# Order of the context stages and priority of the weight splits in a hybrid RWKV-7 and Conformer backbone

## The chip, the cores and the metric

The kernel runs on one core of one Trainium2 chip. The metric is the device time of one execution in microseconds (us). Three executions of the kernel before took 1431.3, 1439.53 and 1440.98 us; the median is 1439.53.

## The reference

The kernel computes two layers over 512 latent tokens of width 1024, with 256 context tokens as a prefix, all in float32. Layer 0 normalises both streams, projects them with one wide matrix, runs RWKV-7 time mixing in both directions beside a short gated convolution, and projects back. Layer 1 is a Conformer convolution module on the latent tokens. What matters here is the even layer, cut to its core:

```python
def even_mixer(h, hc, ...):
    rc, kc, vc, ... = split(hc @ w_in)              # context tokens: keys and values are used
    _, S_f, S_b = rwkv_seq(rwkv_prep(hc, rc, kc, vc), zero, zero, ctx_out=False)
    r, k, v, za, bg, cg, xb, zb = split(h @ w_in)   # latent tokens
    ya, _, _ = rwkv_seq(rwkv_prep(h, r, k, v), S_f, S_b, ...)
    yb = bg * dwconv(cg * xb, sc_w)
    return concat([ya * silu(za), yb * silu(zb)]) @ w_out

def wkv_scan(S, r, decay, k, v, kk, a):             # one step a token, 16 heads of 64
    S = S * w_t + (S @ -kk_t) (kk_t * a_t)^T + v_t k_t^T
    out_t = S r_t
```

The context's scans give only the states S_f and S_b with which the latent scans start. So for a context token only keys and values are projected (and the two low-rank decays), and no output is made.

## The kernel before

**Pairs and stages.** The 16 heads are eight pairs of two, since two heads of 64 fill 128 partitions. The recurrence is worked in chunks of 64 tokens. The context has four chunks, and two pairs of heads are done together as one context state, so there are four context states (0 to 3); the latent tokens have eight chunks and one state for each of eight pairs. These twelve states are the stages of one loop (`for s in range(12)`, the end of the list of calls): stages 0 to 3 run a context state's chain, 4 to 11 a latent one's. Names in the profile that end in c belong to context states, those that end in l to latent ones (AR becomes ARc and ARl).

**What one state needs,** in the order in which its data flow:
- `prep_ctx` (L397): projections of keys and values for two pairs. `project` (L376) loads a weight block of 1024 x 128, multiplies the context rows with it (24 matmuls of 256 columns, tile pck or pcv) and the latent rows (24 of 512, plk or plv), and mixes each token with its neighbours in `shifted` (L368: one ACT and two DVE instructions, L370, L371, L373). The latent result goes to HBM (psp) for later; `prep_lat` (L407) only reads it back.
- `light` (L431): normalised keys, decays and rates, on VectorE and ScalarE with a few matmuls (ssc, lwc, lac), twice over for the two directions. It ends in the tiles AR and BK.
- `heavy` (L589): V transposes and centres the values into UV (`pv`: pvc), B transposes BK (pbc to BKt), A makes the pair products of each chunk (pac or pal) and masks them on VectorE into E (L610), N copies blocks of E into Nt, O is for latent states alone.
- `solve` (L653): 31 double steps on VectorE alone (L667, L669), a triangular inverse of all chunks at once, after a transpose of Nt.
- `merge` (L672): two transposes on VectorE and two groups of 64 small matmuls (uh<-amc, uh<-kdmc) that complete the inverse in E. It takes buffers of light (tags kd, a, P, one buffer each).
- the chain: `chain_ctx` (L698) or `chain_lat` (L749), the sequential part, chunk after chunk. One step of the context's chain is two or three groups of 16 matmuls (zoc, zoc<-cx), copies on ScalarE, 16 matmuls into uh and four instructions on VectorE that give the next state H.

**Weights.** All projections are float32 by three passes: each weight half (128 x 512) is loaded by SyncE's queue into a raw buffer (L125), cast on ScalarE to a high half (L128), and the rest subtracted on VectorE into a low half (L129). `w_half` (L352) does this; there are two raw buffers, and three of each half. A projection's two psum banks are mm0 and mm1 in turn, one buffer each.

**Fills.** `fills(x)` (L908) are projections that no one needs soon: receptances `project(p, 0)` (plr) and gates `gate` (L797, pza), which go to HBM for the latent stages. FILL_R and FILL_Z say which belong to which x: fills(0) R0, R1, Z0; fills(1) Z1 to Z3; fills(2) R2; fills(3) R3, Z4 to Z7; fills(4) R4 to R7. `conv_branch(0)` with four projections follows the last context stage.

**What sets the order.** The program is scheduled when it is built: an instruction is placed on its engine when its inputs and buffers are ready, and of several ready ones that which was written first goes first. So the written order is a priority, and later work moves up into gaps. On the chip each engine runs its list in the placed order. Some dependencies are written by hand: `pinned` keeps the written order within a group of matmuls, `anchored` puts parts of light and heavy behind steps of the running chain (LIGHT_AFTER, HEAVY_AFTER).

The written order of a stage is a string of letters in STAGE: O the latent bonus, F fills(s + 1), P prep of state s + 2, L light of s + 2, S solve of s + 1, M merge of s + 1, H heavy of s + 2, C the convolution branch. It stands behind the chain of stage s and ahead of that of s + 1. Before the loop, states 0 and 1 are prepared in the same manner, with fills(0).

Of the kernel before, what the change touches and what calls it, by code (L numbers as in the profile page):

```python
# [11 lines left out]
ALU = mybir.AluOpType  # L12
# [18 lines left out]
HEAVY_AFTER = ((3, None, 3, 2), (5, None, None, None))  # L31
CONV_AFTER = (0, 2, 7, 6)
PA_ORDER = ((0, 1), (1, 0), (1, 1), (0, 0))
HEAVY = ("VBOAN", "ANBV")
STAGE = ("OFPLSMH", "OSPLMHFC")
FILL_R = (0, 0, 2, 3, 4, 4, 4, 4)
FILL_Z = (0, 1, 1, 1, 3, 3, 3, 3)
ZR = (slice(0, 64), slice(64, 128))
# [13 lines left out]
def kernel(ctx: ExitStack, tc: tile.TileContext, I: dict, out: bass.AP):  # L52
# [62 lines left out]
    w_in = I["ev_w_in"][0]  # L115
    wo = I["ev_w_out"][0]
    ORDER = list(range(8, 16)) + list(range(8))
    env = {"lo": V}

    def bank(name, tag):  # L120
        return ps.tile([P, 512], F32, tag=tag, name=name, bufs=2 if tag in ("at", "zo") else 1)
# [1 line left out]
    def hilo(src, raw, hi, lo, eng=nc.sync):  # L123
        if eng:
            eng.dma_start(raw if len(src.shape) == 2 else raw.rearrange("p (k c) -> p k c", c=src.shape[2]), src)  # L125
        else:
            raw = src
        S.copy(hi, raw)  # L128
        env["lo"].tensor_tensor(out=lo, in0=raw, in1=hi, op=ALU.subtract)  # L129
        return hi, lo  # L130
# [53 lines left out]
    def ch3(t, x=CH):  # L184
        return t.rearrange("p (c x) -> p c x", x=x)
# [166 lines left out]
    def w_half(src, name):  # L352
        raw = wp.tile([P, 512], F32, tag="wr", name="wr" + name, bufs=2)
        hi, lo = (wp.tile([P, 512], F32R, tag="w" + x, name=f"w{x}{name}", bufs=3) for x in "hl")
        return hilo(src, raw, hi, lo)

    def load_w(cb, name):
        lo_for(name)
# [32 lines left out]
    def state(lat, x):  # L391
        ps_ = [x] if lat else [2 * x, 2 * x + 1]
        m = SEQ // len(ps_)
        return {"lat": lat, "nm": ("l" if lat else "c") + str(x), "p": x,
                "parts": [(p, slice(j * m, (j + 1) * m)) for j, p in enumerate(ps_)]}

    def prep_ctx(b, between=None):  # L397
        st = state(False, b)
        for which in (1, 2):
            st["rkv"[which]] = t = w("rkv"[which] + "_", "rkv"[which] + st["nm"])  # L400
            for p, cs in st["parts"]:
                project(p, which, t[:, cs])
                if between:
                    between()
        return st
# [183 lines left out]
    def heavy(st, an=None):  # L589
        ha = (None,) * 4 if an is None else HEAVY_AFTER[an["lat"]]  # L590
        lat, nm = st["lat"], st["nm"]
        v_ = st["v"]
        UV = buf("UV", st)
        E = buf("E", st)
        st["UV"], st["E"], st["BKt"] = UV, E, [buf("BKt", st, z) for z in range(2)]

        def pa():
            for gi, (z, g) in enumerate(PA_ORDER if lat else ((0, 0), (1, 0))):
                with anchored(an, ha[gi if lat else 2 * gi]):
                    AR, BK = st["AR"][z], st["BK"][z]  # L600
                    m, x = (4, P) if lat else (8, CH)
                    c0 = m * g
                    pas = [ch3(ps_at(f"pa{nm}{z}{g}{h}"), x) for h in range(2)]
                    go = pinned(st["ev"] if lat else ())
                    st["ev"] = []
                    for c in range(m):
                        for h in (1, 0):
                            go(pas[h][:, c, :], kb(BK, h, c0 + c), AR[ZR[h], c0 + c, 0:x])
                    for h in range(2):
                        st["ev"].append(V.tensor_tensor(  # L610
                            out=E[:, h, z * NLAT + c0 : z * NLAT + c0 + m, :], in0=pas[h],
                            in1=maskE[:, z * (1 + h) : z * (1 + h) + 1, 0:x].to_broadcast([P, m, x]), op=ALU.mult))

        def pb():
            for z in range(2):
                pbs = [ch3(ps_at(f"pb{nm}{z}{h}")) for h in range(2)]
                go = pinned(st["ev"] if lat else ())
                st["ev"] = []
                for c in range(NLAT):
                    for h in (1, 0):  # L620
                        go(pbs[h][:, c, :], kb(st["BK"][z], h, c), ident[ZR[h], ZR[h]], op=tr)
                for h in range(2):
                    st["ev"].append(S.copy(st["BKt"][z][:, :, ZR[h]], pbs[h]))

        def nt():
            for h in range(2):
                for b in range(2):
                    rs = slice(64 * (1 - h) + 32 * b, 64 * (1 - h) + 32 * b + 32)
                    S.copy(Nt[rs], E[rs, h, :, 32 * b : 32 * b + 32])

        def pv():
            pv = ch3(ps_at(f"pv{nm}"))
            for c in range(NLAT):
                for h in range(2):
                    mm(pv[ZR[h], c, :], v_[ZR[h], c * CH : (c + 1) * CH], ctr[ZR[h], ZR[h]], True, True)
            for z in range(2):
                for h in range(2):
                    src = pv[ZR[h]].rearrange("p (j c) x -> p j c x", j=2)
                    dst = UV[ZR[h], z * NLAT : (z + 1) * NLAT, ZR[h]].rearrange("p (j c) x -> p j c x", j=2)
                    S.copy(dst, src if lat or not z else src[:, :, ::-1, :])  # L640

        def po():
            if lat:
                bon = st["bon"]
                pb = ps_at("pbon" + nm)
                mm(pb, blk, bon, True, True)
                V.scalar_tensor_tensor(out=bon, in0=pb, scalar=0.5, in1=v_, op0=ALU.mult, op1=ALU.mult)

        st["po"] = po
        for x in HEAVY[lat]:  # L650
            {"A": pa, "B": pb, "N": nt, "V": pv, "O": po}[x]()

# [262 lines left out]

    sts = [prep_ctx(0, rest)]
    lora(*first, rest)
    light(sts[0])
    rest()
    heavy(sts[0])  # L920
    rest()
    solve(sts[0])
    merge(sts[0])
# [1 line left out]
    sts.append(prep_ctx(1, rest))  # L925
    light(sts[1])
    heavy(sts[1])
    fills(0)
    for s in range(12):
        st = sts[s]  # L930
# [6 lines left out]
        if s == 11:  # L937
            finish(st)
            break
        for x in STAGE[s >= 4]:  # L940
            if x == "S":
                solve(sts[s + 1])
            elif x == "M":
                merge(sts[s + 1])
            elif x == "O":
                if sts[s + 1]["lat"]:
                    sts[s + 1]["po"]()
            elif x == "P" and s < 10:
                sts.append(prep_ctx(s + 2) if s < 2 else prep_lat(s - 2))
            elif x == "L" and s < 10:  # L950
                light(sts[s + 2], st)
            elif x == "H" and s < 10:
                heavy(sts[s + 2], st)
            elif x == "F":
                fills(s + 1)
                if s >= 4:
                    finish(st)
            elif x == "C":
                conv_branch(s - 3, st["anchor"])
                if s == 10:  # L960
                    rs.close()
                    op = rs.enter_context(tc.tile_pool(name="op", bufs=1, reuse_waits="tile", side="right"))
                    env["lo"] = V
# [375 lines left out]
```

## Time and profile before

The profiled execution took 1434.6 us; its span from the first to the last instruction is 1432.5 us. Times in the profile are counted from the span's start. For orientation:

| Stretch, us | What runs |
|---|---|
| 0 to 122 | normalisation, modulation, low-rank inputs, first keys and values |
| 122 to 227 | states 0 and 1 prepared, fills(0) |
| 227 to 520 | context stages; their chains run at 227, 320, 395 and 456 |
| 520 to 950 | eight latent stages of about 54 us |
| 950 to 1432 | output projection, Conformer layer |

| Engine | Busy, us | Share of the span |
|---|---|---|
| TensorE (PE) | 1376.7 | 96% |
| TensorE weight loads (PEld) | 1008.3 | 70% |
| VectorE (DVE) | 983.0 | 69% |
| ScalarE (ACT) | 749.5 | 52% |

A matmul's busy time in the profile is longer than the distance to the next one, since they are pipelined; the distance between starts tells the pace. PEclk is the clock that was granted to TensorE, 1.00 being full speed.

### The profile page before, as it was taken

What the parts mean: (1) busy time and instruction counts of PE and PEld (TensorE: products, weight loads), DVE (VectorE), ACT (ScalarE), POOL (GpSimd) and SP (SyncE); (2) the same over time, 40 slices, a digit from 0 to 9 for tenths busy, and PEclk for the clock granted to TensorE, in tenths of its full rate; (3) what the DMA queues carried; (4) which work ended last, traced back from release to release, by engine and by line L of the source; (5) the groups of instructions that cost most, each with busy time, mean ns of one, the idle gap of its engine ahead of it and who ended that gap; (6) DMA issues with size and microseconds to landing.
All of it is one profiled execution on the core that took longest, in us unless ns stands there. A gap on an engine that the chain in (4) does not pass through costs nothing.

```text
span 1432.5 us, 29756 instructions
## 1 busy us (share of the span) xinstructions
PE 1376.7 (96%) x11921; PEld 1008.3 (70%) x11921; DVE 983.0 (69%) x2294; ACT 749.5 (52%) x1516; POOL 117.9 (8%) x246
## 2 busy tenths in 40 slices
PE   6899999999998998999999999999999999999998
PEld 1464677878776766666666666778777777788886
DVE  2675597568678989999999999656745545544333
ACT  4636355254555666756667565456753423464322
POOL 2023210000101101011010100010000000000000
PEclk9999999979898999999999999999999999999999
DMA  9754433222322221222222312358813303133322
GB/s 322 226 177 161 156 111 97 92 60 61 93 87 75 82 81 60 77 75 71 83 77 68 98 43 92 110 174 321 265 45 118 119 9 109 59 100 92 103 89 88
DMA packets 137626, 158.54 MB, mean 111 GB/s; under 512 B 15375, under 2 KB 104143, under 8 KB 137369
## 3 DMA queue, kind: packets, MB, share of 16 engines
q1 hardware_dynamic: 121104, 106.47, 23.7%
q0 software_dynamic: 15312, 48.99, 10.5%
q8 instruction: 94, 1.54, 0.4%
q10 hardware_dynamic: 1072, 1.19, 0.2%
q14 instruction: 44, 0.36, 0.1%
HBM read 138.33 MB, written 18.28 MB: 109 GB/s over the span
## 4 chain that ended last, share of the span: by engine, by line
PE 63%; DVE 14%; ACT 5%; issue 2%; DMA 0%; DVEq 0%; ACTq 0%
PE pu L57 12%; PE pz L57 6%; PE f L57 6%; PE o L57 5%; PE uh L57 4%; PE zol L57 4%; PE pcg L57 3%; PE pxb L57 3%; PE pza L57 3%; DVE E L610 2%; PE plk L57 2%; PE zoc L57 2%; PE pzb L57 2%; PE plv L57 1%; PE pac L57 1%
## 5 line engine op out<-in xcount | busy, mean ns | idle before, releaser
L57 PE MATMUL o<-wh,y 128*128 128x512 f32 x248 | 79.6, 397 | 0.0
L667 DVE TENSOR_TENSOR xtmpl<-Xl,Yl 128x126 f32<-128x126 f32 (+22 forms) x248 | 62.3, 251 | 2.8
L669 DVE TENSOR_TENSOR Yl<-Yl,xtmpl 128x126 f32<-128x126 f32 (+22 forms) x248 | 62.3, 251 | 2.7
L1152 ACT CAST ah<-a 64x512 fp32r<-64x512 f32 x32 | 19.8, 619 | 72.2 <-DVE a L1147 71.8
L57 PE MATMUL pal<-ARl,BKl 64*128 64x128 f32 x512 | 46.3, 300 | 10.7 <-DVE E L610 4.9
L57 PE MATMUL zol<-UV,E 64*64 64x64 f32 (+1 forms) x1024 | 54.2, 221 | 0.0
L57 PEld LDWEIGHTS o<-wh,y 128*128 128x128 f32 x248 | 45.9, 188 | 9.5
L57 PEld LDWEIGHTS pal<-ARl,BKl 64*128 64x128 f32 x512 | 36.4, 194 | 22.2 <-issue 7.2
L57 PE MATMUL zol<-Hl,ARl 64*64 64x64 f32 x896 | 50.2, 230 | 1.2 <-DVE Hl L782 1.0
L775 ACT COPY UV<-uh 64x128 f32<-64x128 f32 x128 | 33.2, 260 | 33.1 <-PE uh L57 25.6
L57 PE MATMUL o<-wl,y 128*128 128x512 f32 x124 | 49.4, 398 | 1.2 <-DVE wl L129 1.2
L57 PEld LDWEIGHTS zol<-Hl,ARl 64*64 64x64 f32 x896 | 35.0, 133 | 21.2 <-issue 17.0
L129 DVE TENSOR_TENSOR wl<-wr,wh 128x1024 fp32r<-128x1024 f32 x28 | 34.2, 1222 | 19.7 <-ACT wh L128 17.0
L57 PEld LDWEIGHTS uh<-UV,BKt 128*64 128x64 f32 x704 | 26.3, 137 | 28.7 <-ACT UV L775 23.0
L1147 DVE TENSOR_TENSOR a<-pu,a 128x512 f32<-128x512 f32 x16 | 11.0, 690 | 50.5 <-PE pu L57 48.2
L57 PEld LDWEIGHTS zol<-UV,E 64*64 64x64 f32 (+1 forms) x1024 | 42.4, 136 | 2.8 <-ACT UV L775 2.1
L610 DVE TENSOR_TENSOR E<-pal,maskE 128x512 f32<-128x512 f32 x64 | 42.9, 685 | 2.0 <-PE pal L57 1.2
L1107 DVE SCALAR_TENSOR_TENSOR pr<-px,dbe,What 119x512 f32<-119x512 f32 x32 | 22.6, 746 | 26.8 <-PE px L57 26.8
L782 DVE SCALAR_TENSOR_TENSOR Hl<-uh,PCl,HPl 128x64 f32<-128x64 f32 x112 | 26.5, 277 | 19.5 <-PE uh L57 8.6
L128 ACT CAST wh<-wr 128x1024 fp32r<-128x1024 f32 x28 | 29.6, 1056 | 19.7 <-DMA wr<-in_ev_w_out_dram 10.3
L886 POOL DMA_DIRECT2D mwr<-in_mod_w_dram x56 | 29.8, 537 | 112.8 <-PE uh L57 67.7
L57 PE MATMUL uh<-UV,BKt 128*64 128x64 f32 x704 | 36.3, 232 | 2.5 <-ACT UV L775 2.5
(947 smaller groups left out, 4230.9 us busy)
## 6 DMA issues: line engine op xcount, KB each, us to landing
mwr<-in_mod_w_dram POOLq DMA_DIRECT2D x56, 256.0 KB, 3.5
wr<-in_ev_w_out_dram SPq DMA_DIRECT2D x28, 512.0 KB, 5.1
ectx<-in_mod_w_dram SPq DMA_DIRECT2D x12, 512.0 KB, 5.2
wrk<-in_ev_w_in_dram SPq DMA_DIRECT2D x16, 256.0 KB, 3.1
wrv<-in_ev_w_in_dram SPq DMA_DIRECT2D x16, 256.0 KB, 4.1
wrr<-in_ev_w_in_dram SPq DMA_DIRECT2D x16, 256.0 KB, 2.7
wrza<-in_ev_w_in_dram SPq DMA_DIRECT2D x16, 256.0 KB, 2.8
wrcg<-in_ev_w_in_dram SPq DMA_DIRECT2D x16, 256.0 KB, 2.8
```

The lines of the kernel that those rows point to most:

```text
L57: return T.matmul(o, lhsT, rhs, start=start, stop=stop)
L128: S.copy(hi, raw)
L129: env["lo"].tensor_tensor(out=lo, in0=raw, in1=hi, op=ALU.subtract)
L610: st["ev"].append(V.tensor_tensor(out=E[:, h, z * NLAT + c0 : z * NLAT + c0 + m, :], in0=pas[h], in1=maskE[:, z * (1 + h) : z * (1 + h) + ...
L667: V.tensor_tensor(out=tv, in0=X[:, :i, i : i + 1].to_broadcast([P, i, m]), in1=Y[:, i : i + 1, c0:].to_broadcast([P, i, m]), op=ALU.mult)
L669: V.tensor_tensor(out=Y[:, :i, c0:], in0=Y[:, :i, c0:], in1=tv, op=ALU.add)
L775: u_ = S.copy(UV[ZR[1 - h], i : 2 * nch - i : 2 * nch - 1 - 2 * i, ZR[h]], uh[ZR[1 - h], 0:2, :])
L782: h_ = V.scalar_tensor_tensor(out=Hn[:, z, :], in0=uh[:, 2 + z, :], scalar=PC[z][:, i : i + 1], in1=HP[:, z, :], op0=ALU.mult, op1=ALU.add)
L886: nc.gpsimd.dma_start(mws[q], I["mod_w"][layer, kt * P : (kt + 1) * P, c0 : c0 + 512])
L1107: V.scalar_tensor_tensor(out=pr[s][:NPROD], in0=px[s][:NPROD], scalar=dbe[:, 0:1], in1=What[:, n * 512 : n * 512 + 512], op0=ALU.add, op1= ...
L1147: V.tensor_tensor(out=a, in0=pp[1], in1=a, op=ALU.mult)
L1152: S.copy(ahl[s][hr], a[hr])
```

## The change

Three things are changed, all around the context stages.

1. **The written order.** STAGE has a string of its own for stages 0 and 1: K (keys of state s + 2), L, S, M, H, V (its values), v (its pv), F. Before, the fills stood first, then keys and values together, then the small work. In stages 2 and 3 the fills move from ahead of P to the end. The latent stages' string is the same.
2. **pv.** It is taken out of heavy for the context states and called behind it; at that place the values are there. For states 0 and 1 it follows heavy at once.
3. **Priority of the splits.** From the low-rank part's end until stage 4, `w_half` runs in `tc.high_priority()`: load, cast and subtraction of a weight half are placed ahead of all other ready work of their engines.

```diff
-HEAVY = ("VBOAN", "ANBV")
-STAGE = ("OFPLSMH", "OSPLMHFC")
+HEAVY = ("BAN", "ANBV")
+STAGE = ("KLSMHVvF", "OPLSMHF", "OSPLMHFC")
...
-        return hilo(src, raw, hi, lo)
+        with tc.high_priority() if env["first"] else nullcontext():
+            return hilo(src, raw, hi, lo)
...
-    def prep_ctx(b, between=None):
-        st = state(False, b)
-        for which in (1, 2):
+    def prep_ctx(b, between=None, st=None, kinds=(1, 2)):
+        st = st or state(False, b)
+        for which in kinds:
...
-        st["po"] = po
+        st["po"], st["pv"] = po, pv
...
     lora(*first, rest)
+    env["first"] = True
     light(sts[0])
     rest()
     heavy(sts[0])
+    sts[0]["pv"]()
...
     heavy(sts[1])
+    sts[1]["pv"]()
     fills(0)
...
-        for x in STAGE[s >= 4]:
+        env["first"] = s < 4
+        for x in STAGE[(s >= 2) + (s >= 4)]:
...
+            elif x == "K":
+                sts.append(prep_ctx(s + 2, kinds=(1,)))
+            elif x == "V":
+                prep_ctx(s + 2, st=sts[s + 2], kinds=(2,))
+            elif x == "v":
+                sts[s + 2]["pv"]()
             elif x == "P" and s < 10:
-                sts.append(prep_ctx(s + 2) if s < 2 else prep_lat(s - 2))
+                sts.append(prep_lat(s - 2))
```

More of the change, by code (lines that the diff above doesn't have):

```diff
@@ L117 @@
     ORDER = list(range(8, 16)) + list(range(8))
-    env = {"lo": V}
+    env = {"lo": V, "first": False}
     def bank(name, tag):
@@ L591, in heavy @@
         lat, nm = st["lat"], st["nm"]
-        v_ = st["v"]
         UV = buf("UV", st)
@@ L631, in pv @@
         def pv():
-            pv = ch3(ps_at(f"pv{nm}"))
+            pv, v_ = ch3(ps_at(f"pv{nm}")), st["v"]
             for c in range(NLAT):
@@ L646, in po @@
                 mm(pb, blk, bon, True, True)
-                V.scalar_tensor_tensor(out=bon, in0=pb, scalar=0.5, in1=v_, op0=ALU.mult, op1=ALU.mult)
-        st["po"] = po
+                V.scalar_tensor_tensor(out=bon, in0=pb, scalar=0.5, in1=st["v"], op0=ALU.mult, op1=ALU.mult)
+        st["po"], st["pv"] = po, pv
         for x in HEAVY[lat]:
```

## The prediction

> **What bounds the kernel now.** I read the head of the page first, then the busy time by stage, then the stretches around each drop of the clock, and last the order of time on single engines inside the worst stage.
>
> ```profile
> span 1432.5 us, 29756 instructions
> PE 1376.7 (96%) x11921; PEld 1008.3 (70%) x11921; DVE 983.0 (69%) x2294; ACT 749.5 (52%) x1516; POOL 117.9 (8%) x246
> PEclk9999999979898999999999999999999999999999
> ```
>
> TensorE is busy nearly all the time, so a gain has to come from the few places where it idles or runs slow. The clock row has three weak slices after the start, all between 280 and 480 us. That is the context stage. The next rows cut it by what happens there: chain of pair 0, bulk projections, small work, and so on. The columns are length, then busy us of PE, PEld, DVE, ACT and POOL, then granted clock and DMA.
>
> ```profile
> 253.00:287.00 34.00, 34.00 (x195) 29.95 (x194) 17.85 (x42) 10.15 (x18) 2.16 (x4) 1.00 0.30 94
> 287.00:320.00 33.00, 29.62 (x336) 23.48 (x337) 22.59 (x43) 19.89 (x40) 1.62 (x3) 0.79 0.22 64
> 320.00:346.00 26.00, 26.00 (x301) 20.57 (x302) 19.80 (x64) 13.82 (x35) 0.55 (x1) 0.93 0.14 42
> ...
> 363.00:395.00 32.00, 30.09 (x334) 22.55 (x332) 23.09 (x44) 20.53 (x41) 5.66 (x10) 0.84 0.32 94
> 395.00:425.00 30.00, 30.00 (x305) 22.77 (x305) 23.68 (x72) 15.78 (x39) 1.62 (x3) 0.94 0.26 77
> 425.00:456.00 31.00, 26.21 (x255) 20.07 (x253) 29.38 (x70) 16.74 (x29) 5.66 (x10) 0.84 0.29 91
> 456.00:484.00 28.00, 27.03 (x352) 19.56 (x351) 22.18 (x68) 18.65 (x44) 1.20 (x3) 0.93 0.23 71
> 484.00:520.00 36.00, 33.61 (x315) 26.10 (x314) 34.92 (x82) 21.41 (x36) 4.59 (x8) 1.00 0.32 92
> 520.00:573.00 53.00, 48.42 (x609) 33.29 (x609) 45.91 (x141) 36.42 (x89) 5.59 (x10) 1.00 0.20 62
> ```
>
> The pattern repeats. A block of bulk runs with TensorE solid while VectorE is half idle (253 to 287: the keys and values of pair 2; DVE 17.85 of 34). Then the small work (light, merge, heavy) runs nearly bare (287, 363 and 425): TensorE idles, and the clock is down. The drops themselves, each with the 3.41 us ahead of it:
>
> ```profile
> 302.92:306.33 3.41, 1.22 (x18) 0.87 (x18) 3.41 (x6) 3.08 (x6) 0.54 (x1) 1.00 0.00 0
> 306.33:323.39 17.06, 16.72 (x221) 15.40 (x222) 7.12 (x12) 4.92 (x10) 0.54 (x1) 0.50 0.21 63
> 381.42:384.83 3.41, 2.04 (x83) 1.86 (x80) 3.33 (x7) 2.91 (x6) 0.55 (x1) 1.00 0.32 88
> 384.83:398.49 13.66, 13.66 (x145) 11.55 (x144) 5.69 (x9) 3.42 (x7) 0.55 (x1) 0.50 0.26 79
> 442.86:446.27 3.41, 0.55 (x9) 0.58 (x11) 3.41 (x10) 1.26 (x3) 0.56 (x1) 1.00 0.26 87
> 446.27:459.93 13.66, 13.20 (x185) 10.12 (x183) 9.70 (x16) 4.57 (x9) 1.63 (x3) 0.50 0.30 98
> ```
>
> A short stretch with little PE work is paid for with 14 to 17 us at half clock, while PE is busy throughout. What half clock costs is seen on one group, the 30 pair products: 2.00 us at full clock, 3.67 in the first spell. Then what PE waited for ahead of the drops:
>
> ```profile
> 163.15 2.00 PE L57 MATMUL pac<-ARc,BKc 64*128 64x64 f32 x30
> ...
> 303.95 0.50 PE L57 MATMUL pck<-hctx,whk 128*128 128x256 f32 x2 [1.40 <-ACT whk L128]
> 306.67 1.92 PE L57 MATMUL uh<-amc,ectx 32*32 32x32 f32 x64 [1.36 <-DVE amc L676]
> 316.24 3.67 PE L57 MATMUL pac<-ARc,BKc 64*128 64x64 f32 x30
> ...
> 382.96 1.20 PE L57 MATMUL uh<-amc,ectx 32*32 32x32 f32 x64 [1.37 <-DVE amc L676]
> 445.72 1.61 PE L57 MATMUL pal<-ARl,BKl 64*128 64x128 f32 x16 [3.83 <-DVE Yc L669]
> ```
>
> Each time PE either waits for a split (first row) or stands in front of small work whose operand is still on VectorE, with no projection left to run meanwhile. The projections were missing because their splits came late:
>
> ```profile
> 442.30 0.62 ACT L128 CAST whr<-wrr 128x512 fp32r<-128x512 f32 x1 [2.34 <-DMA wrr<-in_ev_w_in_dram]
> ...
> 259.22 0.18 DVE L669 TENSOR_TENSOR Yc<-Yc,xtmpc 128x16 f32<-128x16 f32 x1
> ...
> 304.29 1.12 DVE L675 STREAM_TRANSPOSE kdmc<-Yc 128x512 f32<-128x512 f32 x1
> ...
> 308.19 0.68 DVE L129 TENSOR_TENSOR wlk<-wrk,whk 128x512 fp32r<-128x512 f32 x1
> ...
> 384.49 0.68 DVE L129 TENSOR_TENSOR wlza<-wrza,whza 128x512 fp32r<-128x512 f32 x1
> ```
>
> The low halves at 308.19 and 384.49 arrive after the drop has been earned (306.33), or 0.3 us ahead of it; at 442.30 the cast waits for a load that itself waited for its raw buffer. One more thing is seen: solve of pair 1 is done at 259.4, but its merge begins at 304.29. Merge takes its buffers (kd, a, P) behind light of pair 2, and light had to wait for all four projections of the block.
>
> **The change, part by part.**
>
> *Order in stages 0 and 1.* Nothing is removed; every matmul, copy and DMA is the same. Ahead of light there are now two key projections instead of three gate fills, two keys and two values. Values, pv and the fills follow heavy and take the place of missing filler. So the time comes from PE's own losses in the small sections and cannot exceed them. I count them from the rows above:
> - Clock: 17.06 + 13.66 + 13.66 = 44.4 us at 0.50 cost at most 22.2 us.
> - Idle PE: 3.4 (33.00 − 29.62) + 1.9 + 4.8 + 1.0 + 2.4 = 13.5 us over 287 to 520.
>
> The sections at 287 and 363 are those that gain the values and the fills: clock 8.5 + 6.8 and idle 3.4 + 1.9, together 20.6 us. The one at 425 and what hangs on it (clock 6.8, idle 4.8 + 1.0 + 2.4) is 15.0 us.
>
> *What fills them.* One matmul of a projection starts every 0.23 us at full clock (first two rows); the other rows are stages again, with the instructions of one tile alone: plr at 287, pza at 363, pck at 287.
>
> ```profile
> 258.31 0.39 PE L57 MATMUL plk<-hlh,whk 128*128 128x512 f32 x1
> 258.54 0.39 PE L57 MATMUL plk<-hll,whk 128*128 128x512 f32 x1
> ...
> 287.00:320.00 33.00, 7.11 (x24) 4.19 (x24) 1.46 (x2) 0.71 (x1) 0.79 0.22 64
> ...
> 363.00:395.00 32.00, 5.67 (x17) 3.33 (x17) 0.00 (x0) 0.00 (x0) 0.84 0.32 94
> ...
> 287.00:320.00 33.00, 3.89 (x19) 3.08 (x19) 0.00 (x0) 0.00 (x0) 0.79 0.22 64
> ```
>
> A value projection has 24 of these and 24 of half the width, 8.3 us; two make 16.6, and the gate fills of stage 0 (3 x 24 x 0.23) another 16.6. Inside the section at 287 there are now 24 matmuls of plr (5.5 us) and 19 narrow ones of pck (19 x 0.12, half the width: 2.3), at 363 as many of plr and 17 of pza. So there is four times the filler in stage 0, and about no idle time should be left; in stage 1 it is 16.6 + 5.5 us against 9.4. I take five sixths of 20.6: **−17 us**. (Bounds: 0, if the filler is placed but the small work then waits behind it; −20.6.)
>
> *Stages 2 and 3.* There the fills only change place with light, merge and heavy, and latent pairs need no projection first. What helps at 425 is the split's priority alone. VectorE is busy 29.38 of 31 us there, so its own queue may keep the section long whatever PE does. I take half: **−7.5 us** (bounds 0 and −15.0).
>
> *Splits first.* Each half costs 0.62 on ACT and 0.68 on DVE as before, only earlier. It can now stand ahead of a link of the chain. The chain of pair 0 had this filler:
>
> ```profile
> 227.00:253.00 26.00, 18.63 (x70) 12.00 (x69) 1.36 (x2) 1.16 (x2) 1.00 0.25 78
> ```
>
> That is 70 matmuls of pza, 16 us, or 6 halves of 12; over four chains 24 halves, each delaying a link by 0 to 0.68, so 0 to +16 us. ACT is free for nearly half of a chain's stretch (13.82 of 26 busy at 320) and DVE for a quarter, and the splits lie between the links already, so I go to the low end: **+1.5 us**. SyncE's queue has the same loads; light's eight small loads can stand behind a weight load that waits for its raw buffer, but they are issued long before light (the eight of pair 3, first and last below, for a light after 363), so I cost that at nothing; without that lead it would be one half's 2.8 us (12 x 0.23) of matmuls.
>
> ```profile
> 293.13 0.53 SPq L456 DMA_DIRECT2D lwc3lwl<-in_ev_w_dram  x1
> ...
> 298.33 0.60 SPq L457 DMA_DIRECT2D lwc3h<-in_ev_a_dram  x1
> ```
>
> *pv behind heavy; the stretch ahead of 227 us.* pv is read first by the chain two stages on, so its move costs nothing while it ends before that; if not, the chain waits for its 32 matmuls of the kind that the chain itself has 64 of in a step, about a microsecond. In the opening the splits of pair 1 also go first, but PE has nothing to give back there:
>
> ```profile
> 122.00:165.00 43.00, 42.98 (x268) 21.92 (x263) 22.21 (x46) 23.62 (x48) 13.33 (x25) 1.00 0.55 172
> ```
>
> I take 0 (bounds −3 and +3, the 2.8 us of one half, rounded).
>
> **Sum.** −17 − 7.5 + 1.5 = −23. The profiled execution took 1434.6 us (span 1432.5, 2.1 around it), so 1411.6, say **1412 us**. The median shown is 1439.5, the lowest 1431.3: the profiled one lies between, and 1412 is 1.9% below the median. Does VectorE have room? Its busy time from 253 to 520 is fixed; at 287, 363 and 395 it is busy 22.59 of 33, 23.09 of 32 and 23.68 of 30. Shortened by 20 us, those stages and the block would reach what the latent stage at 520 already runs at (45.91 of 53). It has room.
>
> The Trainium skill ("TensorE: Matmul & The Clock Gate", "Part 1: The HAM clock gate" and "HAM oscillation — how this bites in real kernels") names a window of 3.4 us, and the trace agrees: the spells are 5 and 4 times 3.41. It also says that only an idle gap longer than that lowers the clock. Here the trace disagrees: the first drop follows gaps of 1.40 and 1.36 us, with PE busy 1.22 of 3.41. By the skill's rule filling such gaps would gain no clock in two of the spells; the gain would be some 13 us smaller, where the second rival below ends. I go by the rows.
>
> **The rivals.**
> 1. *Everything is recovered* (both losses, 35.6 us): **1399 us**. For it: filler is ample in stage 0 and later splits are ready wherever PE has a hole. Against: VectorE at 425.
> 2. *The filler runs dry on its banks.* A projection needs mm0 or mm1, and its evacuation (L370 to L373) is now written behind light, solve, merge and heavy on VectorE. If VectorE never finds room, PE gets one projection (8.3 us) per section and stops; the section at 287 has 5.5 us and the narrow ones already. Then each of two sections gains about 1 us of idle and one of three spells goes (7 us): −2 − 7 + 1.5, **1427 us**, and with a longer wait up to no change at all. For it: DVE runs 3.41 of 3.41 ahead of two drops. Against: DVE's holes in the section at 287, which the second row makes 1.9 us and the first two of up to 3.7:
>
> ```profile
> DVE ectx L610 <- PE pac L57: 5.2, 2, 3.7
> ...
> DVE ARc L551 <- ACT Pc L527: 1.9, 1, 1.9
> ```
>
> 3. *The bulk comes in one block behind the small work* (slower). If light, merge and heavy follow each other closely in the written order, the values start only after the pair products, where the fills of 287 and 363 now start ahead of them. The bulk that hides there now is then on top: 5.5 + 2.3 + 9.4 = 17 us, and the spells stay: **1452 us**. The chain of the next pair is written behind that block, and so waits for it. It decides itself at one point: whether the first plv of a pair starts before its pac. For it: a block like this stands at 253. Against: the small work waits for ACT and DVE between its steps (the 1.4 us above), and ready matmuls go there.
>
> That the change does not do what it says would be seen as plv ahead of the pair's ssc and lwc; the order is written in the stage's list, so I give it no chance of its own.
>
> **How the numbers follow.** A measurement of this kernel tells about 1% from no change (the runs shown spread by 0.7%). Forecast (1400 to 1425): 0.50. First rival (below 1400): 0.17. Second (1425 to 1445): 0.20. Third: 0.13. Faster by over 1% is below 1425: 0.67; within: 0.20; slower: 0.13. The range holds the first case down to 1392 (all losses and 7 us more, what one spell costs) and the second up to 1440.
>
> **What would show it.** Right: no stretch of half clock between 280 and 480 us, plv matmuls between the pair's lwc and pac, merge of pair 1 well before 290 us, the first latent chain (zol) starting some 20 us ahead of 520. Wrong: a spell of 13 to 17 us still in each stage with PE standing before a projection that waits for L371 or L373 (second rival); plv solid after pac (third); or PE full and at full clock, yet zol no earlier, which would mean that PE's losses were not what set the stage's length.

## The result and the profile after

The changed kernel takes **1421.16 us** (median of 20 runs, 1417.83 to 1432.03); beside it the kernel before took 1438.24 us (20 runs, 1431.3 to 1440.98). The ratio is **0.9901**, with a 95% interval of 0.9887 to 0.9915: faster by 1.0%, 17 us.

The two profiled executions show only a third of that: 1428.73 us after against 1434.6 before. The one of after lies 7.6 us above its median, the one of before 3.6 below its own. So the first question is in what the runs of one kernel differ. Each run lists its span and its granted clock, and from these I work out two numbers for each: **lost clock**, (1 − clock) × span, and **net**, the time less the lost clock. For the profiled execution of after, (1 − 0.987) × 1426.4 = 18.5 us lost, net 1428.7 − 18.5 = 1410.2; for that of before, (1 − 0.982) × 1432.5 = 25.8 and 1408.8. One execution of e1 below (1445.8 us), over 1.5% above that kernel's fastest, counts as a slow one and is left out of its numbers. Over all runs:

| Kernel | Runs | Median us | Lost clock, mean | Net, mean |
|---|---|---|---|---|
| before (beside the experiments) | 74 | 1437.2 | 26.4 (17.1 to 34.5) | 1410.5 (standard deviation 2.4) |
| after | 20 | 1421.2 | 11.2 (7.1 to 20.0) | 1411.8 (standard deviation 1.5) |

Within the 20 runs of after, time goes with lost clock at a slope of 0.90 (correlation 0.94), while net hardly moves. Within the 74 runs of before the slope is only 0.59 (correlation 0.81): a microsecond of lost clock need not cost a whole one, so net is a rough measure, and small differences of it between kernels that lose different amounts prove little. Between the kernels lost clock fell by 15.2 us and net rose by 1.3 (by these means the change is −13.9 us; by medians it is more, since after has a few long runs). A comparison that does without net: at a granted clock of 0.986 to 0.988, 13 runs of before took 1432.5 us on average and four of after 1429.5. So **nearly the whole gain is granted clock**; at the same clock the two kernels are some 3 us apart. These are means of many runs; a single pair could have shown anything from nothing to 23 us.

The head of the profile after, to be read against the one shown ahead:

```profile
span 1426.4 us, 29742 instructions
PE 1370.3 (96%) x11921; PEld 1002.7 (70%) x11921; DVE 982.2 (69%) x2294; ACT 748.5 (52%) x1516; POOL 118.2 (8%) x246
PEclk9999999889999999999999999999999999999999
```

The same 11921 matmuls; the slices near 380 and 450 us are full again, the two from 250 to 321 are not. By stage, in the columns of before (length, busy us of PE, PEld, DVE, ACT and POOL, then clock and DMA):

```profile
255.00:298.00 43.00, 41.13 (x366) 32.49 (x366) 29.70 (x67) 22.41 (x44) 1.62 (x3) 0.76 0.19 56
298.00:315.00 17.00, 17.00 (x101) 14.12 (x96) 14.98 (x46) 7.28 (x13) 1.62 (x3) 1.00 0.39 124
315.00:342.00 27.00, 27.00 (x321) 21.77 (x320) 16.21 (x54) 12.56 (x33) 1.08 (x2) 1.00 0.21 65
342.00:382.00 40.00, 38.46 (x413) 30.55 (x411) 31.89 (x63) 25.91 (x50) 6.33 (x11) 1.00 0.29 87
382.00:405.00 23.00, 22.83 (x285) 16.55 (x283) 22.13 (x66) 19.66 (x46) 2.59 (x5) 1.00 0.29 81
405.00:440.00 35.00, 32.10 (x353) 24.34 (x349) 31.51 (x80) 17.12 (x32) 4.21 (x8) 0.95 0.35 105
440.00:462.00 22.00, 21.88 (x268) 15.72 (x269) 20.86 (x61) 18.70 (x44) 2.26 (x5) 1.00 0.22 64
462.00:488.00 26.00, 22.18 (x187) 17.12 (x189) 23.89 (x63) 12.44 (x25) 4.13 (x8) 1.00 0.39 115
488.00:514.00 26.00, 25.06 (x254) 20.43 (x249) 14.81 (x21) 10.89 (x19) 1.08 (x2) 1.00 0.32 93
```

PE's idle time is length less busy: 1.9 + 1.5 + 0.2 + 2.9 + 0.1 + 3.8 + 0.9 = 11.3 us, against 13.5 before over the same work. So idle time hardly fell. The clock column shows where the gain is: 1.00 in seven of the nine rows. What is left of half clock, each spell with the stretch ahead of it:

```profile
273.52:276.93 3.41, 2.14 (x49) 1.46 (x46) 3.37 (x6) 3.04 (x7) 1.06 (x2) 1.00 0.36 87
276.93:297.41 20.48, 20.48 (x201) 16.93 (x193) 7.98 (x11) 4.67 (x8) 0.02 (x1) 0.50 0.11 37
...
430.53:433.94 3.41, 2.50 (x81) 2.00 (x77) 2.51 (x5) 2.78 (x5) 1.07 (x2) 1.00 0.38 93
433.94:437.35 3.41, 3.41 (x18) 2.27 (x18) 3.07 (x10) 1.97 (x4) 0.00 (x0) 0.50 0.43 145
...
553.41:560.23 6.82, 5.66 (x29) 4.30 (x31) 6.49 (x28) 2.47 (x4) 0.00 (x0) 0.50 0.28 79
```

In the context 23.9 us at half clock are left of 44.4, and 6.8 have come up in the first latent stage. The big spell sets this execution apart: its 20.48 us cost 10.2 us, and the median run lies 7.6 below.

The rows also show when a spell comes. The spells of one execution start on one grid of 3.413 us: in before 306.33, 384.83 and 446.27 lie 23.0 and 18.0 steps apart, in after 276.93, 433.94 and 553.41 lie 46.0 and 35.0. I count PE's busy time in the steps of that grid from 223 to 950 us, in the fourteen profiles of this document, where the clock is full. All 23 steps with 1.66 us or less were followed by half clock, 10 of 83 with 1.77 to 2.50 us, and none of 2772 with more. So filler is enough where it keeps PE busy for over 2.5 us of every 3.41; below that a spell is a chance, and below 1.7 it came every time.

What PE did just ahead of it, and at the same place one stage later:

```profile
263.27 0.40 PE L57 MATMUL plv<-hlh,whv 128*128 128x512 f32 x1
...
274.01 0.71 PE L585 MATMUL pbc<-ident,BKc 64*128 64x64 f32 x16 [0.34 <-ACT BKc L561]
275.64 0.50 PE L57 MATMUL plv<-hlh,whv 128*128 128x512 f32 x1 [0.92 <-DVE lv L374]
276.53 1.68 PE L57 MATMUL uh<-amc,ectx 32*32 32x32 f32 x64
278.14 3.25 PE L57 MATMUL pac<-ARc,BKc 64*128 64x64 f32 x28
...
362.62 0.50 PE L57 MATMUL plv<-hlh,whv 128*128 128x512 f32 x1 [0.82 <-DVE lv L374]
```

Values (plv) run from 263.27, ahead of the pair products (pac, 278.14): the filler is where the order puts it. But at 275.64 the second projection has its split and waits 0.92 us for its **bank**, which the evacuation on VectorE (L374) frees. At 362.62 it waits 0.82 us for the same, and no spell follows there. The step ahead of the big spell, with 2.14 us busy, is one of those in which it is a chance. VectorE ahead of it:

```profile
273.88 1.11 DVE L675 STREAM_TRANSPOSE kdmc<-Yc 128x512 f32<-128x512 f32 x1
274.88 0.71 DVE L374 SCALAR_TENSOR_TENSOR lv<-plv,hmu,lv 128x511 f32<-128x511 f32 x1
```

The transpose of merge stands in front of the evacuation. The same row shows merge of pair 1 at 273.88 where it was at 304.29: it no longer waits for four projections. Last, the latent matmuls uh<-Ol (one group for each latent chunk; first and last start), of before and of after:

```profile
L57 PE MATMUL uh<-Ol,E x512: 218/218/268, 523.2 to 950.4; 64*64 64x64 f32 x171
```

```profile
L57 PE MATMUL uh<-Ol,E x512: 218/218/268, 514.2 to 944.9; 64*64 64x64 f32 x171
```

The first is 9.0 us earlier. The context's spells cost 22.2 us before and 11.9 now, 10.3 less. So up to the first latent chain the net is 523.2 − 22.2 = 501.0 and 514.2 − 11.9 = 502.3; the latent stages take 427.2 net before, and after 430.7 less 3.4 for the spell at 553, 427.3. In this pair of profiles nothing but clock moved.

### The profile page after: what moved, and what is told of

Same layout as the page of the kernel before. It is cut to its first block, busy times and chain, and to the rows that moved or that the text cites. A ratio compares the mean times of both kernels' runs of the same rounds, so it can differ in the third digit from the quotient of the medians.

```text
span 1426.4 us, 29742 instructions
## 1 busy us (share of the span) xinstructions
PE 1370.3 (96%) x11921; PEld 1002.7 (70%) x11921; DVE 982.2 (69%) x2294; ACT 748.5 (52%) x1516; POOL 118.2 (8%) x246
## 3 DMA queue, kind: packets, MB, share of 16 engines
q1 hardware_dynamic: 121104, 106.47, 23.9%
## 4 chain that ended last, share of the span: by engine, by line
PE 52%; DVE 9%; ACT 4%; issue 2%; DMA 1%; POOL 0%; DVEq 0%; SPq 0%; ACTq 0%; POOLq 0%
PE pu L57 12%; PE pz L57 6%; PE f L57 6%; PE o L57 5%; PE zol L57 4%; PE pcg L57 3%; PE uh L57 3%; PE pxb L57 3%; DVE E L610 2%; PE pzb L57 1%; PE pc L57 1%; PE px L57 1%; PE pbg L57 1%; DVE Yl L669 1%; DVE xtmpl L667 1%
## 5 line engine op out<-in xcount | busy, mean ns | idle before, releaser
L128 ACT CAST wh<-wr 128x1024 fp32r<-128x1024 f32 x28 | 29.5, 1055 | 21.5 <-PE o L57 13.0
L57 PEld LDWEIGHTS uh<-Ol,E 64*64 64x64 f32 x512 | 19.9, 133 | 26.8 <-ACT Ol L769 20.4
```

The costliest lines, as they stand in the source:

```text
L57: return T.matmul(o, lhsT, rhs, start=start, stop=stop)
```

## The experiments

**Theory:** the written order puts ready projections into the small work's gaps, and what that saves is granted clock. **Rivals:** the splits' priority does it; or a filler is there but PE stands before its bank, so that only an earlier evacuation helps; and, by pieces, the fills or pv and not the values. The expectations below call the theory C; rival O is that light waits for keys alone, so that merge and the chain start earlier, and rival S that late splits alone were at fault. Every ratio is to the kernel before, beside the same runs. The table collects the runs; the sections below say what each was for.

| Kernel | Runs | Median us | Ratio (95%) | Lost clock | Net |
|---|---|---|---|---|---|
| e1 priority alone | 11 | 1436.25 | 0.9979 (0.9957 to 1.0002) | 23.3 | 1411.0 |
| e2 order alone | 6 | 1425.33 | 0.9915 (0.9892 to 0.9938) | 14.0 | 1411.2 |
| e3 stages 2, 3 as before | 6 | 1417.62 | 0.9877 (0.9853 to 0.9900) | 11.8 | 1407.4 |
| e4 evacuation first | 4 | 1416.87 | 0.9858 (0.9836 to 0.9879) | 7.8 | 1408.7 |
| e5 only values behind | 5 | 1422.57 | 0.9907 (0.9894 to 0.9920) | 10.2 | 1412.6 |
| e6 only fills behind | 12 | 1436.64 | 1.0002 (0.9980 to 1.0025) | 22.7 | 1414.3 |
| e7 e3 and e4 together | 4 | 1417.69 | 0.9874 (0.9860 to 0.9888) | 7.1 | 1410.7 |
| e8 pv alone | 11 | 1436.14 | 1.0001 (0.9988 to 1.0014) | 25.7 | 1410.7 |
| e9 values behind, no more | 10 | 1428.26 | 0.9949 (0.9932 to 0.9966) | 18.7 | 1409.7 |
| e10 priorities in all stages | 8 | 1429.56 | 0.9954 (0.9935 to 0.9973) | 13.2 | 1415.9 |
| e11 filler of stage 3 later | 6 | 1424.80 | 0.9924 (0.9907 to 0.9942) | 12.8 | 1411.8 |
| e12 old order, evacuation first | 12 | 1427.99 | 0.9946 (0.9924 to 0.9968) | 21.5 | 1407.4 |

### Priority alone, order alone

e1 is after with the old order and pv in heavy again; e2 is after without the priority:

```diff
-STAGE = ("KLSMHVvF", "OPLSMHF", "OSPLMHFC")
+STAGE = ("OFPLSMH", "OSPLMHFC")            # e1, with all that goes with it
...
-        with tc.high_priority() if env["first"] else nullcontext():
-            return hilo(src, raw, hi, lo)
+        return hilo(src, raw, hi, lo)        # e2
```

> Splits first, in the written order of before. Theory C (the gain is granted clock: the time is about 1410 us plus the clock that is lost): the stretches at 287 and 363 keep their place, but the projection of the next stage has its weights in time, so at least one of the three spells of half clock goes; mean clock 0.987 to 0.990, 1424 to 1430 us. Rival O (order: merge and the chain of pair 1 can start earlier because light waits for keys alone): without the order no gain, 1436 to 1440 us, and merge of pair 1 still at 300 us or later. Rival S (late splits alone were the fault): the whole gain, 1418 to 1423 us.

> The written order of after, splits at their own place in it. Theory C: the values and fills stand behind light, solve, merge and heavy, and so do their casts and subtractions on ScalarE and VectorE, so the filler is not there when the small work has its holes; two or three spells stay, clock 0.980 to 0.986, 1430 to 1440 us. Rival O: the gain comes with the order, 1418 to 1424 us. Rival S: no gain or a loss, 1438 us or more.

Order alone has the gain, as far as the intervals can tell (0.9892 to 0.9938 against 0.9887 to 0.9915); priority alone can't be told from nothing. Both went against theory C as it was written down, which gave early splits alone 1424 to 1430 us and the order alone 1430 or more; e1 lies within rival O's range and e2 1.3 us beside it, which the next section takes up. Why early splits don't help by themselves is seen in e1's trace, first the stretch ahead of its large spell and the spell, then PE in that stretch:

```profile
305.88:309.29 3.41, 1.14 (x18) 0.82 (x18) 3.41 (x6) 2.69 (x6) 0.52 (x1) 1.00 0.02 5
309.29:333.19 23.90, 23.90 (x245) 18.95 (x245) 9.37 (x17) 8.07 (x17) 0.69 (x2) 0.50 0.11 34
```

```profile
307.88 0.78 PE L585 MATMUL pbc<-ident,BKc 64*128 64x64 f32 x16 [1.81 <-ACT BKc L561]
309.12 0.66 PE L57 MATMUL plk<-hlh,whk 128*128 128x512 f32 x1 [0.46 <-DVE lr L374]
```

There is a projection (plk, at 309.12), but it stands 0.46 us before a bank that VectorE frees with the evacuation of the receptance (lr, L374), and the small work ahead of it 1.81 us before a copy. A split that is ready early is no filler while its bank is full; e12 below tests this.

### Which part of the order

e5 keeps only the values behind the small work, e6 only the fills, e8 is the kernel before with only pv moved, e9 is e5 with the old string for stages 2 and 3 and without priority:

```diff
-STAGE = ("KLSMHVvF", "OPLSMHF", "OSPLMHFC")
+STAGE = ("FKLSMHVv", "OPLSMHF", "OSPLMHFC")   # e5
+STAGE = ("KVLSMHvF", "OPLSMHF", "OSPLMHFC")   # e6
+STAGE = ("OFPLSMH", "OSPLMHFC")               # e8: pv called behind heavy
+STAGE = ("FKLSMHVv", "OFPLSMH", "OSPLMHFC")   # e9: and w_half without priority
```

> As after, but in stages 0 and 1 the fills stand first again; only the values (and pv) are behind the small work. Called net: a run's time less the clock that it lost, (1 - clock) x span. Theory C: what counts is that the small work has bulk written behind it; 16.6 us of values is enough for a section whose holes are a few us, so the lost clock stays near that of after (11 us), net 1409 to 1413, 1419 to 1425 us. Rival O (light's early start counts: it must not wait for more than the keys): the fills ahead delay light by up to 16.6 us in stage 0, so lost clock 20 us or more, 1430 us or more.

> As after, but in stages 0 and 1 the values stand ahead of light again; only the fills are behind. Theory C: in stage 0 the fills are 16.6 us and suffice, in stage 1 they are 5.5 us, so a spell can come back there: lost clock 12 to 20 us, net 1409 to 1413, 1423 to 1431 us. Rival O: light waits for keys and values as in before, so the whole gain goes: lost clock 24 us or more, 1434 us or more.

> Before, with pv alone moved behind heavy in the context stages. The prediction's step: nothing, 1436 to 1440 us, lost clock 25 to 30. Rival (its 32 matmuls and four copies on ScalarE stood ahead of the operands of the pair products, so heavy comes sooner): up to 4 x 0.6 us of ScalarE per stage off the small section, a spell fewer, 1428 to 1434 us.

> The least of the change: in stages 0 and 1 the values and pv behind the small work, fills first and stages 2 and 3 in the old order, no priority for splits. If the values as filler carry the gain: lost clock 10 to 15 us, net 1407 to 1412 us, 1419 to 1426 us. If their splits must also come first: lost clock 20 us or more, 1430 us or more.

The values carry it: e5 has the whole gain, as theory C had it, and e6 none, where C had some. Rival O fails on e5. In the profiles, merge of pair 1 begins at 273.9 us in after, 290.5 in e5 and 291.1 in e6: e5 keeps the gain with a merge as late as that of e6, which has none. By the written order both have 33 us of bulk ahead of light and 16.6 behind the small work in stage 0; in stage 1 e5 has 16.6 behind it and e6 only the 5.5 of one receptance, which may be why. Where e6 loses its clock stays open, and so does its net, 3.8 us above that of before: its profiled execution took 1425.3 us, far less than its median.

pv alone changes nothing in the time, as expected (e8). e9 has half of the gain, between its two expectations; it differs from e5 in the priority and in the order of stages 2 and 3, and no run separates these two. Its profiled execution has two spells, at both ends of the context:

```profile
225.17:235.41 10.24, 10.24 (x88) 8.29 (x89) 3.47 (x5) 3.94 (x7) 0.00 (x0) 0.50 0.18 51
436.80:450.45 13.65, 12.62 (x182) 10.45 (x183) 9.50 (x16) 3.75 (x8) 1.08 (x2) 0.50 0.25 80
```

Between them, where the values were moved, there is none. The first has a counterpart in e2 (6.83 us at 228.79) and e8 (6.83 at 228.21), the two other versions with pv moved and no priority. Ahead of it PE waits for VectorE in the pair products, 2.13 us in e9, 1.90 in e2 and in e8:

```profile
226.80 0.43 PE L57 MATMUL pac<-ARc,BKc 64*128 64x64 f32 x2 [2.68 <-DVE ectx L609]
```

The profile of before, where pv stood ahead of the pair products, and those of all versions with the priority have neither this wait of some 2 us nor a spell there. So the end of the opening, at 225 to 229 us, is the one place where a use of the priority is seen: with pv moved, it keeps a projection ready there. That rests on one profile of each version.

### Stages 2 and 3

e3 is after with the old string for stages 2 and 3:

```diff
-STAGE = ("KLSMHVvF", "OPLSMHF", "OSPLMHFC")
+STAGE = ("KLSMHVvF", "OFPLSMH", "OSPLMHFC")
```

> As after, but stages 2 and 3 have their fills ahead of the small work again. If the moved fills there bring what the prediction gave them (half of 15 us together with the splits), 1425 to 1430 us and a spell between 420 and 460 us. Theory C: the splits' priority suffices in these stages, since every later fill can be pulled forward; the same as after, 1418 to 1424 us.

Undoing this part costs nothing, as theory C expected: lost clock 11.8 against 11.2, and net 1407.4 against 1411.8, 4.4 less (standard deviations 1.6 and 1.5, six runs and twenty). By the ratios alone the two versions overlap. The rows uh<-Ol of e3, and the only spell that its profile has in the context:

```profile
L57 PE MATMUL uh<-Ol,E x512: 218/218/366, 513.2 to 935.4; 64*64 64x64 f32 x171
```

```profile
441.71:448.54 6.83, 6.83 (x101) 5.56 (x95) 5.04 (x8) 1.49 (x4) 1.09 (x2) 0.50 0.11 39
```

Net of 3.4 us the first latent chain starts at 509.8, 7.5 later than after's 502.3, and the latent stages take 422.2 less another 3.4 for a spell at 541, 418.8 against 427.3. The sum is 928.6 against 929.6. The fills themselves (plr, pza) end before 505 us in both; what has moved are projections of the next convolution branch, which follow in the written order. Those of pcg up to 514 us (PE, PEld), after and then e3:

```profile
405.00:514.00 109.00, 6.53 (x24) 4.28 (x24) 0.58 (x1) 0.98 0.33 96
```

```profile
405.00:514.00 109.00, 11.71 (x40) 6.97 (x40) 0.58 (x1) 0.97 0.32 94
```

Sixteen more, 3.7 us at 0.23, are done in e3 while the context still runs, and are missing from the latent stages. For the other 4 us of the 7.5 no row was found. So, as far as rows show, this part of the change shifts work across the border of the stages, and it gains no time.

### Evacuation first

e4 is after with the three instructions that free the bank in the same priority as the splits:

```diff
     def shifted(pl, res, p, which):
         j, n = which * 8 + p, pl.shape[1]
-        S.activation(res, pl, AF.Copy, scale=omu[:, j : j + 1])
...
+        with tc.high_priority() if env["first"] else nullcontext():
+            S.activation(res, pl, AF.Copy, scale=omu[:, j : j + 1])
...
```

e7 is e4 with e3's string, e12 is e1 (old order) with this edit.

> As after, and the three instructions that empty a projection's bank (copy on ScalarE, two mixes on VectorE) also go first in the context stages. Theory C: the spell at 277 us in the profile of after was set off by 3.4 us in which PE was busy 2.14 us, with one wait of 0.92 us for the bank; without that wait the spell never comes and every run is like the fast ones of after: 1414 to 1419 us, spread under 6 us, clock 0.994 or more. Rival (the evacuations now stand ahead of light, merge and the chain on VectorE, which is the true limit of these stages): no gain or a loss, 1420 to 1428 us at the same or a better clock.

> The two variants that were ahead of after together: stages 2 and 3 in the old order, and evacuations first. If the 4 us of net (1407.4 against 1411.8) and the smaller clock loss (7.8 against 11.2) add: net 1404 to 1407, lost clock 8, 1411 to 1415 us. If the net gain of the evacuations (1408.7) was the same time as that of the old order: net 1408, 1415 to 1418 us.

> The written order of before, with splits and evacuations both first. In e1 (splits alone) PE stood in front of a bank at 309 us (plk waits 0.46 us for DVE L374, behind a wait of 1.81 us for ScalarE) and then ran 23.9 us at half clock. If the bank was what kept the ready filler from running: lost clock 8 to 14 us instead of 24, 1418 to 1425 us. If the order is needed because only it puts enough bulk behind the small work: lost clock 20 us or more, 1430 us or more. Net 1409 to 1412 us by both.

e4 is the best version: 0.9858, its interval wholly below that of after (0.9836 to 0.9879 against 0.9887 to 0.9915). Its stage at 255, its clock row, and PE where after waited for lv:

```profile
PEclk9999999999999999999999999999999999999999
```

```profile
255.00:298.00 43.00, 41.29 (x410) 32.69 (x410) 36.10 (x86) 27.28 (x51) 2.16 (x4) 1.00 0.25 75
...
429.69:433.10 3.41, 3.41 (x21) 1.63 (x23) 2.80 (x5) 1.73 (x3) 0.43 (x1) 0.50 0.20 67
```

```profile
277.47 0.50 PE L57 MATMUL plv<-hlh,wlv 128*128 128x512 f32 x1
```

The projection at 277.47 follows without a wait, 410 matmuls pass in that stage instead of 366, and of the context's half clock 3.41 us are left. The median, 1416.9, is in theory C's range (1414 to 1419), and the runs spread by 5.4 us instead of 14.2. But that the wait for the bank set off the spell is not shown. e3 has the wait of after at this place, and no spell follows:

```profile
277.95 0.50 PE L57 MATMUL plv<-hlh,whv 128*128 128x512 f32 x1 [0.92 <-DVE lv L374]
...
274.46:277.87 3.41, 2.24 (x40) 1.82 (x38) 3.41 (x6) 1.96 (x5) 0.27 (x1) 1.00 0.28 77
```

And e4 still idles 1.7 us in its stage (1.9 in after), for other operands; in its step of the grid from 276.09 PE is busy 2.30 us. All three profiles are in the range in which a spell is a chance. What is shown is the sum over e4's runs: 3.4 us less lost clock and 3.1 less net than after. e7, by the second of its expectations, gains nothing beyond e4: the two edits do not add.

In e12 the evacuation with the splits' priority, in the old order, brings about half (0.9946): about 5 us of clock and 3 of net. That lies between its two expectations: the bank was part of what kept early splits from helping, and the order is still needed. In its profile there is no spell at all from 255 to 490 us. Then 3.41 us follow at 494.64 and these:

```profile
488.00:520.00 32.00, 25.23 (x336) 17.68 (x333) 25.83 (x76) 13.93 (x28) 2.17 (x4) 0.76 0.23 69
...
508.29:525.36 17.07, 14.65 (x202) 9.28 (x194) 10.36 (x43) 8.09 (x22) 1.07 (x2) 0.50 0.19 52
```

```profile
507.61 1.48 PE L57 MATMUL uh<-aml,E 32*32 32x32 f32 x64 [2.00 <-DVE aml L678]
```

PE idles 6.8 of 32 us there and waits for VectorE's transpose in merge (aml, L678) with nothing ready beside it. Two more spells, 10.2 and 6.8 us, follow in the latent stages at 566 and 672. That the bulk written first has been used up first, so that the last sections are bare, fits this and is not tested.

### Filler and priorities further on

e11 is e4 with the convolution branch that follows the last context stage (four projections) put a stage later; e10 is e4 with both priorities kept through the latent stages:

```diff
+        if s == 4:
+            conv_branch(0, st["anchor"])    # e11, no longer at s == 3
...
-        env["first"] = s < 4
+        env["first"] = True                  # e10
```

> As e4, with the first convolution branch (four projections, 22 us of matmuls in a block where VectorE is half idle) written behind the first latent chain, so that it is filler there. Theory that the kernel's net time is set by TensorE's work alone: the block only moves, net within 2 us of e4's 1408.7. Rival (block and latent chain overlap, since the chain leaves TensorE gaps): net 1395 to 1404 us. Rival on the other side: VectorE is full in the latent stages and takes the branch's 8 us on top: net 1412 to 1417 us.

> As e4 (evacuations and splits first), and that priority kept on through the latent stages. If the small spells of the first latent stages (about 546 us) come from late splits of the convolution branch: lost clock 5 to 7 us, 1412 to 1416 us. If VectorE sets these stages (50.4 of 54 us busy), splits and evacuations ahead of the chain's links only delay it: net 1412 us or more, 1419 us or more.

Both give back what e4 had over after, and e10 more than that. By e11 the block neither just moves (net within 2 us of 1408.7) nor overlaps (1404 or less): net is 1411.8, at the edge of the rival on the other side (1412 to 1417). e11 takes filler from the end of the context, and a spell comes up there in its profile, 13.65 us with PE busy 10.73:

```profile
484.95:498.60 13.65, 10.73 (x181) 7.54 (x181) 7.75 (x15) 7.79 (x15) 1.01 (x2) 0.50 0.14 41
```

e10 came out as its second expectation had it: 5.4 us more lost clock than e4 and 7.2 more net. In the two profiles PE's waits for VectorE between 515 and 950 us sum to 16.3 us in e10 and 8.6 in e4, its waits for ScalarE to 5.3 and 5.1. So the net is in waits for VectorE; that they come of splits and evacuations done ahead of a chain's links is argued.

## Why the prediction was right and where it was wrong

The forecast was 1412 us, inside a range of 1392 to 1440; the measured median is 1421.2. That is in the band that the prediction gave to its forecast (1400 to 1425), but nearer to the second rival's 1427 than to 1412.

**Right: what the gain is, and the size of its larger part.** The clock's share of the forecast was five sixths of 8.5 + 6.8 and half of 6.8: 12.8 + 3.4 = 16.2 us. Measured over all runs it is 15.2. That small work with a projection beside it keeps its clock came out so, and pv and the splits' own cost show nothing in the time (e8; e1 isn't slower than before). The order was rightly given the larger part: e2 alone 0.9915, e1 alone 0.9979. That the clock's sum agrees so well is in part luck. In the profiled execution stages 0 and 1 gain 8.5 + 6.8 − 10.2 = 5.1 us of clock where 12.8 were forecast, and stages 2 and 3 gain 6.8 − 1.7 = 5.1 where 3.4 were. The half for stages 2 and 3 stood for the splits' priority, and e2 has nearly the whole gain without it. And the opening, set at 0, gains and loses: pv's move without the priority brings a spell at 225 to 229 us there.

**Wrong: the idle term.** The same fractions were applied to idle PE: five sixths of 3.4 + 1.9 and half of 4.8 + 1.0 + 2.4, 4.4 + 4.1 = 8.5 us. Measured by net it is nothing, which rose by 1.3 us; at equal clock it is 3 us at most. By the means the change is −13.9 us where −23.2 was forecast (−16.2 − 8.5 + 1.5). Of the 9.3 missing, 1.0 is clock and 9.8 idle time (8.5 and 1.3), less the 1.5 set against the splits, which are within that net. The step that failed is "about no idle time should be left". In stages 0 and 1 idle went from 5.3 us to 1.9 + 1.5 + 0.2 = 3.6; in stages 2 and 3 from 8.2 to 2.9 + 0.1 + 3.8 + 0.9 = 7.7. The filler was four times as much as before, but PE waits on other things now. The three largest waits of PE over the context after, by who ended them (total, times, longest):

```profile
PE pal L57 <- DVE E L610: 2.8, 3, 2.0
PE plv L57 <- DVE lv L374: 1.7, 2, 0.9
PE pbl L585 <- ACT BKt L623: 1.4, 2, 0.8
```

The second row is the banks, as the second rival said, and small; the others are small work of the latent pairs waiting for VectorE and ScalarE in stages 2 and 3. For those stages the prediction itself said that the fills only change place, and then took half of the idle time all the same, for the splits' priority. e3 has the priority there without the moved fills, and its net is the lower one. And the 1.7 us won in stages 0 and 1 do not arrive: 501.0 and 502.3 net at the first latent chain.

**The rivals.** Everything recovered (1399) did not come. The second rival's mechanism is there, with the rows that it named (a projection that waits for L374, which is L373 in the kernel before), but it costs little by itself: after's lost clock is 11.2, and that of e4, where the bank is freed earlier, 7.8. That is worth 1421.2 − 1416.9 = 4.3 us here by the medians, 6.4 by the means, and not the 15 that separated its 1427 from the forecast. In the old order it is worth about as much (e1 to e12: 0.9979 to 0.9946, with intervals that overlap). The third rival's block did not form: values start at 263.27 and the first pair products come at 278.14.

**The signs.** Merge of pair 1 ahead of 290 us and values ahead of pac: as forecast. No half clock between 280 and 480: not so in the profiled execution (20.48 and 3.41 us), nearly so in e4. First latent chain 20 us earlier: 9.0 by uh<-Ol, in an execution with a spell of 10.2 at 277; in e4 it starts at 506.8, 16.4 earlier. (The tile zol, which the prediction names, is no sign of it: its first matmuls, zol<-UV,E, now run long before the chain, at 471.8.)

```profile
L57 PE MATMUL uh<-Ol,E x512: 218/218/267, 506.8 to 928.6; 64*64 64x64 f32 x171
```

**The rule on idle gaps.** The prediction weighed a rule of the Trainium skill ("TensorE: Matmul & The Clock Gate", "HAM oscillation — how this bites in real kernels") by which only idle gaps beyond the window lower the clock, and went by the rows. The runs agree with the rows: spells followed 3.41 us in which PE was busy 2.14 and 2.50 us, with a longest wait of 0.92 us in the first. Closer to them is another section of that page ("A second HAM failure mode: psum-queue depth-cycling"), which tells of a kernel that cycles through its banks and whose short idle times between groups let the clock swing; the wait for lv at 275.64 is of that kind. What the counts above follow, though, is a sum: PE's busy time in one step of the grid, whatever it waits for.

**What stays open.** What decides between 1.77 and 2.50 us of busy time in a step: a spell follows 2.14 us in after at 277 and 2.50 at 434, and none follows 1.91 from 471.49 and 2.00 in the step behind it. And why e12 has half of the gain with much of the lost clock of before (21.5 against 26.4): its net is about 3 us lower, and no row shows where; so is e3's.

## What to carry to other kernels

Split each run's time into lost clock and net before explaining a difference, since a single pair of profiles can show a third of it; compare runs of equal clock as well. Bulk work that is independent of a chain is worth most between the small operations, not ahead of them: keep one ready projection for each section with gaps, and see that its weights and also its bank are free in time: the best version here gives the priority to the instructions that free the bank as well as to those that prepare the weights. Do not count idle time of the critical engine as gained because filler exists; name for each gap which operand ends it.

## What the runs showed of the hardware

- The same program has runs of 1417.8 to 1432.0 us, and the difference is granted clock: 7.1 to 20.0 us lost, net has a standard deviation of 1.5 us. The spell at 277 came behind waits of 0.34 and 0.92 us and cost 10.2; behind waits of 0.33 and 0.92 us at the same place e3 has none.
- Spells of half clock last whole multiples of 3.41 us: 3.41, 6.82, 10.24, 13.65, 17.07, 20.48, 23.90 in the rows above and before. In the two longest PE is busy throughout (20.48 and 23.90), so being busy does not end a spell at once.
- TensorE does not have to be idle for 3.41 us to lose its clock. The stretches ahead of spells had PE busy 1.14 us (e1), 2.14 and 2.50 us (after). On the grid of 3.413 us on which spells start, 23 of 23 steps with PE busy up to 1.66 us led to half clock, 10 of 83 from 1.77 to 2.50, and 0 of 2772 above.
